# First conditioning round in two halves, the second among the first projections' products; later conditioning from the ninth load on

## The chip, the cores and the metric

One core of a Trainium2 chip runs the whole program. The metric is the time of one execution on the device in microseconds (us); lower is better. TensorE does matrix products, VectorE and ScalarE do element-wise work, GpSimd does a little, and SyncE issues nearly all transfers. Products are accumulated in PSUM, eight banks of 128 x 512 floats.

## The reference

A decoder trunk of two residual layers over 256 tokens of 1024 channels, in float32. Each layer computes a conditioning vector of 6 x 1024 values from c, `ada = silu(c) @ ada_w[l] + ada_b[l]`, split into shift, scale and gate for the token mixer and for the channel mixer, and then:

```
h = rmsnorm(x, norm_mix_g[l]) * (1 + sc1) + sh1
x = x + g1 * token_mixer(h, ...)
h = rmsnorm(x, norm_ffn_g[l]) * (1 + sc2) + sh2
x = x + g2 * (swiglu(h) if l is even else moe_swiglu(h))
```

The token mixer multiplies h by one wide matrix w_in (nine projections side by side, the first 512 columns being the queries hq of a gated linear recurrence and the next 512 its forget gates hf). It runs the recurrence and a differential softmax attention on the results, projects each of them, weighs them with sigmoid gates and applies w_out. The channel mixer is a dense SwiGLU in layer 0 and a choice of 2 out of 8 experts in layer 1.

## The kernel before

Activations lie transposed: a tile holds 128 channels by 256 tokens, and eight such channel blocks (k = 0 to 7) make the 1024 channels. To keep float32 accuracy at the faster fp32r rate, each operand is split into a high part (ScalarE copy, `wh`, `hh`) and a low part (VectorE difference, `wl`, `hl`), and three products are formed for each pair (`three`, L157). The helper `split` (L146, L148) does that for the weights, 1024 columns at a time. `load` (L120 and L123) fetches 1 MB of weights into one of six `raw` buffers, over SyncE's queue.

Conditioning (`ada_steps`) is done in rounds of 2048 columns, three for each layer. Round (0, 0) gives shift and scale of layer 0's token mixer. A round reads eight blocks of 1 MB, block k holding the rows p * 8 + k of the weights. A block is either multiplied on TensorE with silu(c) as the stationary operand ("t" in the table `ADA`) or accumulated on VectorE ("v", L219 and L221). The last block is followed by a copy of the result row, transposes and the addition of the bias, which turn it into columns. Round (0, 0) is all on TensorE, and its 512 result columns lie in two banks of 256 so that the first half can be finished a little earlier than the second. Even so all eight blocks must have arrived before either half is complete.

While round (0, 0) goes on, x is loaded between the first blocks, transposed (L370, L371), squared and summed (L261, L263, L271), and scaled by the inverse norm (L389). When the round is done, `norm_T` forms high and low parts of h (L299 to L301), and the mixer starts. Its steps come in the order of the string `ORDER`: first "r", the queries' projection, then "f", the forget gates' (both by `proj_T`: two loads each of 8 x 128 x 256 weights, all eight channel blocks accumulated for a group of 128 columns before the next group), then "s", the recurrence's scores (L530 to L565), "i", "q", "k", "g", "v" (projections by `proj_N`, two loads each), the attention "a" and "b", the recurrence's output "o", and four gates "0" to "3". The two branch projections and w_out follow.

The later conditioning rounds are cut into steps, the `fillers`. After each load of the mixer, `fill` may take one of them: the table `DELAYS` says after how many loads the first is taken, `RATES` every how many loads one is taken after that. Layer 0's mixer has 26 such loads, and 17 fillers: the attention's lambdas, and the rounds (0, 1) and (0, 2) of eight steps each. With a delay of 2 they fall on loads 2 to 18. The gate of round (0, 1) and the scale of round (0, 2) are needed when the outputs of w_out are evacuated. The first round does not count its blocks as such loads.

The program is not run in the order in which it is written. A scheduler with a model of the times orders the instructions of each engine, and the order on each queue is then fixed. `issue_after` ties a transfer to come no earlier than a given load in that order; `first_load` lists the mixer's loads from the first on.

Of the kernel before, what the change touches and what calls it, by code (L numbers as in the profile page):

```python
# [8 lines left out]
F32 = mybir.dt.float32  # L9
# [8 lines left out]
P = 128  # L18
D = 1024
# [24 lines left out]
DELAYS = (2, 8, 4, 0)  # L44
# [4 lines left out]
def hybrid_trunk(ctx: ExitStack, tc: tile.TileContext, x, c, ada_w, ada_b, norm_mix_g, norm_ffn_g, w_in, lb_logits,  # L49
# [43 lines left out]
    def ms():  # L93
        return msp.tile([P, 512], F32, tag="ms", name=nm("ms"))
# [97 lines left out]
    def ada_steps(l, r):  # L192
# [5 lines left out]
        halves = 2 if (l, r) == (0, 0) else 1  # L198
# [85 lines left out]
    def norm_T(rb, gain, sc, sh, xr=None):  # L284
# [4 lines left out]
        for part in ((0, 1), (2, 3)) if xr else ((0, 1, 2, 3),):  # L289
            js = slice(part[0], part[-1] + 1)  # L290
            gv, scv, av = (q.rearrange("p (h i) -> p h i", i=4)[:, :, js] for q in (gm, sc, gain))
            v_.scalar_tensor_tensor(gv, scv, 1.0, av, op0=ALU.add, op1=ALU.mult)
            for k in [4 * h + i for h in range(2) for i in part]:
                h, i = k // 4, k % 4
                hi, lo = hs[h], ls[h]
                val = small([P, S], "val", pool=prep)
                if xr:
                    x_ = xr[h][:, i, :]
                    s_.activation(hi[:, i, :], x_, AF.Identity, bias=sh[:, k:k + 1], scale=gm[:, k:k + 1])  # L299
                    v_.tensor_scalar(val, x_, gm[:, k:k + 1], sh[:, k:k + 1], op0=ALU.mult, op1=ALU.add)  # L300
                    v_.tensor_tensor(lo[:, i, :], val, hi[:, i, :].bitcast(F32), op=ALU.subtract)  # L301
                    continue
                v_.scalar_tensor_tensor(val, xT[h][:, i, :], gm[:, k:k + 1], rb[:, :S], op0=ALU.mult, op1=ALU.mult)
                s_.activation(hi[:, i, :], val, AF.Identity, bias=sh[:, k:k + 1])
                v_.scalar_tensor_tensor(lo[:, i, :], val, sh[:, k:k + 1], hi[:, i, :].bitcast(F32),
                                        op0=ALU.add, op1=ALU.subtract)
        return hs, ls
# [54 lines left out]

    ada = {}
    steps, ada[0, 0] = ada_steps(0, 0)

    def turn_x(t):
        for j in range(2):
            ps = ms()
            for k in range(4):
                t_.transpose(ps[:, k * P:(k + 1) * P], x_in[t][:, (j * 4 + k) * P:(j * 4 + k + 1) * P], ident)  # L370
            v_.tensor_copy(xT[j][:, :, t * P:(t + 1) * P], ps.rearrange("p (k t) -> p k t", k=4))  # L371

    pcol = const.tile([P, R_ALL], F32, name="pcol")
    for n, f in enumerate(steps):
        f()
        if n < NT:
            nc.sync.dma_start(x_in[n], x[0, n * P:(n + 1) * P, :])
            if n:
                nc.sync.dma_start(brows, ada_b.rearrange("l (k p) -> (l k) p", p=P))
        elif n < 2 * NT:  # L380
            turn_x(n - NT)
        elif n == 2 * NT:
            acc = []
            for k in range(KD):
                add_square(acc, k)
            rb = norm_rows(acc)
            xr = [w4("xr").rearrange("p (k t) -> p k t", k=4) for _ in range(2)]
            for k in range(KD):
                v_.tensor_tensor(xr[k // 4][:, k % 4, :], xT[k // 4][:, k % 4, :], rb[:, :S], op=ALU.mult)  # L389
        elif n == 2 * NT + 1:  # L390
            pps = ms()
            t_.transpose(pps[:, :R_QN], rows, ident[:R_QN, :R_QN])
            t_.transpose(pps[:, P:P + 96], brows, ident[:96, :96])
            v_.tensor_copy(pcol[:, :R_QN], pps[:, :R_QN])
            v_.tensor_copy(bcol, pps[:, P:P + 96])
# [54 lines left out]
    def mixer(l, norm, early, rb):  # L450
# [15 lines left out]

        def forget():

            def ev_f(g, ps):
                z, b = scaled(ps)  # L470
                s_.activation(f[:, g, :], z, AF.Sigmoid, bias=b)
                if z is not ps:
                    b = small([P, 1], "zn")
                    v_.tensor_scalar(b, ps[:, S:S + 1], -1.0, None, op0=ALU.mult)
                s_.activation(kq[:, g, :], z, AF.Sigmoid, bias=b, scale=-1.0)
                if l > 0:
                    v_.tensor_scalar(f[:, g, :], f[:, g, :], lbp[:, 0, g:g + 1], lbp[:, 1, g:g + 1], op0=ALU.mult, op1=ALU.add)
                    v_.tensor_scalar(kq[:, g, :], kq[:, g, :], lbp[:, 0, g:g + 1], None, op0=ALU.mult)
            proj_T(W, C_HF, *parts(True), KD, ev_f, 512)
# [8 lines left out]
        def reader():  # L488
            def ev_q(g, ps):
                z, b = scaled(ps)  # L490
                s_.activation(q[:, g, :], z, AF.Identity, bias=b)
            proj_T(W, C_HQ, *parts(True), KD, ev_q, 512,
                   None if l else (0, 1, 4, 5, 2, 3, 6, 7))
# [816 lines left out]
```

## Time and profile before

| | us |
|---|---|
| median of 3 runs | 1531.02 (1530.73 to 1533.77) |
| the profiled execution | 1531.64 |
| its span, first to last instruction | 1528.1 |
| TensorE busy | 1478.0 (97%) |
| VectorE busy | 625.4 (41%) |
| ScalarE busy | 374.2 (24%) |

The 3.5 us between the profiled execution's time and its span lie outside the recorded instructions. Busy time of TensorE counts overlapping, pipelined matmuls; where it is full, the distance between the starts of two matmuls tells its pace. An fp32 matmul is recorded as two, so the 32 matmuls that one pass over the blocks of half a conditioning round needs appear as 64. "Idle before" in brackets is the time that an engine stood still ahead of a row, and behind the arrow is what ended it. Slices in the first 40 us contain the whole of the stretch that the change edits.

### The profile page before, as it was taken

How to read it: one execution, taken by the hardware profiler on the slowest of the kernel's cores; microseconds unless marked ns; L12 is line 12 of the kernel's file. 1: busy time of each engine (PE TensorE's matmuls, PEld its weight loads, DVE VectorE, ACT ScalarE, POOL GpSimd, SP SyncE). 2: the span in 40 equal slices, each digit the busy share in tenths (PEclk: the TensorE clock that was granted, in tenths of full speed). 3: DMA queues.
4: the chain of work that ended last, by engine and by line, in shares of the span. 5: the costliest groups of instructions: out<-in, count | busy, mean ns of one | idle time of the engine just before them, and what ended most of it. 6: DMA issues, size and time to landing. Idle time of an engine off the chain costs nothing. (4 is left out here: it accounts for less than half of the span.)

```text
span 1528.1 us, 29828 instructions
## 1 busy us (share of the span) xinstructions
PE 1478.0 (97%) x12747; PEld 903.9 (59%) x12747; DVE 625.4 (41%) x1028; ACT 374.2 (24%) x618; POOL 36.1 (2%) x34
## 2 busy tenths in 40 slices
PE   5999999999999999999997999999999999999997
PEld 3988999999998899863342423433433434334332
DVE  4898777877688787630112111111021020110111
ACT  3535556544455455310000000000000000000000
POOL 1020100000000110000000000000000000000000
PEclk7999999999999999999998999999999999999999
DMA  9988545678796656869998999999999999999996
GB/s 355 368 302 282 188 140 165 221 241 303 267 333 227 198 186 200 315 244 366 379 363 337 411 417 412 413 415 414 415 414 412 411 418 409 410 415 409 410 413 262
DMA packets 184480, 506.63 MB, mean 332 GB/s; under 512 B 10872, under 2 KB 79108, under 8 KB 167700
## 3 DMA queue, kind: packets, MB, share of 16 engines
q1 hardware_dynamic: 184020, 504.55, 86.5%
q8 instruction: 102, 1.67, 0.4%
q14 instruction: 38, 0.31, 0.1%
q0 software_dynamic: 320, 0.09, 0.0%
HBM read 503.56 MB, written 1.05 MB: 330 GB/s over the span
## 5 line engine op out<-in xcount | busy, mean ns | idle before, releaser
L1064 PE MATMUL mm<-raw,X 128*32 128x512 f32 (+1 forms) x3888 | 440.0, 541 | 6.8 <-PEq L1165 6.4
L1064 PEld LDWEIGHTS mm<-raw,X 128*32 128x32 f32 x3888 | 134.0, 110 | 230.7 <-issue 190.1
L148 DVE TENSOR_TENSOR wl<-raw,wh 128x1024 fp32r<-128x1024 f32 (+1 forms) x188 | 227.1, 1212 | 73.1 <-ACT wh L146 70.8
L146 ACT ACTIVATE wh<-raw 128x1024 fp32r<-128x1024 f32 (+1 forms) x188 | 196.6, 1048 | 174.9 <-PE mm L157 131.6
L1104 PE MATMUL pd<-raw,u 128*32 128x512 f32 x1664 | 214.6, 594 | 2.1 <-DMA raw<-in_moe_w_dram 2.1
L1072 DVE TENSOR_TENSOR sa<-sa,mm 128x512 f32<-128x512 f32 (+1 forms) x32 | 19.9, 621 | 446.9 <-PE mm L1064 397.5
L157 PE MATMUL mm<-hh,wh 128*128 128x256 f32 x576 | 163.9, 285 | 3.3 <-ACT wh L146 3.1
L157 PE MATMUL mm<-hl,wh 128*128 128x256 f32 x576 | 164.5, 286 | 0.0
L157 PE MATMUL mm<-hh,wl 128*128 128x256 f32 x576 | 164.2, 285 | 0.1
L1069 PE MATMUL at<-raw,X 128*32 128x512 f32 (+1 forms) x968 | 161.6, 540 | 0.0
L1071 ACT ACTIVATE sa<-mm 128x512 f32<-128x512 f32 (+1 forms) x32 | 17.4, 544 | 493.8 <-PE mm L1064 476.4
L1104 PEld LDWEIGHTS pd<-raw,u 128*32 128x32 f32 x1664 | 57.3, 110 | 114.3 <-issue 103.6
L157 PEld LDWEIGHTS mm<-hh,wh 128*128 128x128 f32 x576 | 109.7, 190 | 5.6 <-ACT wh L146 3.4
L157 PEld LDWEIGHTS mm<-hl,wh 128*128 128x128 f32 x576 | 109.2, 190 | 0.7 <-issue 0.7
L157 PEld LDWEIGHTS mm<-hh,wl 128*128 128x128 f32 x576 | 109.0, 189 | 0.4 <-DVE wl L148 0.4
L1110 PE MATMUL pd<-raw,u 128*32 128x512 f32 x408 | 84.9, 592 | 0.0
L1069 PEld LDWEIGHTS at<-raw,X 128*32 128x32 f32 x968 | 44.0, 110 | 61.7 <-issue 56.9
L221 DVE SCALAR_TENSOR_TENSOR raw<-raw,cs,raw 128x2048 f32<-128x2048 f32 x32 | 75.1, 2348 | 10.7 <-DMA raw<-in_ada_w_dram 10.7
L1088 ACT ACTIVATE u<-ms 128x512 f32<-128x512 f32 (+1 forms) x32 | 17.4, 544 | 229.7 <-PE ms L1086 229.7
L157 PE MATMUL mm<-wh,hh 128*128 128x512 f32 x160 | 64.6, 404 | 0.0
L157 PE MATMUL mm<-wl,hh 128*128 128x512 f32 x160 | 64.0, 400 | 0.0
L157 PE MATMUL mm<-wh,hl 128*128 128x512 f32 x160 | 63.2, 395 | 0.0
(294 smaller groups left out, 1977.2 us busy)
## 6 DMA issues: line engine op xcount, KB each, us to landing
raw<-in_moe_w_dram SPq DMA_DIRECT2D x240, 1024.0 KB, 14.8
raw<-in_moe_w_dram SPq DMA_DIRECT2D x152, 512.0 KB, 11.4
raw<-in_ada_w_dram SPq DMA_DIRECT2D x47, 1024.0 KB, 5.2
raw<-in_w_in_dram SPq DMA_DIRECT2D x44, 1024.0 KB, 7.5
raw<-in_ffn_w_dram SPq DMA_DIRECT2D x30, 1024.0 KB, 5.3
xT<-in_moe_w_dram SPq DMA_DIRECT2D x40, 512.0 KB, 15.9
raw<-in_w_out_dram SPq DMA_DIRECT2D x8, 1024.0 KB, 5.4
raw<-in_w_branch_a_dram SPq DMA_DIRECT2D x4, 1024.0 KB, 5.1
```

The source lines that it names most:

```text
L146: s_.activation(wh[:, c], r[:, c], AF.Copy)
L148: v_.tensor_tensor(wl[:, c], r[:, c], wh[:, c].bitcast(F32), op=ALU.subtract)
L157: t_.matmul(ps, lhsT=lhs, rhs=rhs, start=first and i == 0, stop=last and i == 2)
L221: v_.scalar_tensor_tensor(got["acc"], raw, cs[:, k:k + 1], got["acc"], op0=ALU.mult, op1=ALU.add)
L1064: t_.matmul(ups[m][q:q + 32, :n], lhsT=xp[:, k, 32 * s:32 * s + 32], rhs=rhs[m][h], start=k == 0, stop=k == KD - 1)
L1069: t_.matmul(ups[2][q:q + 32, :n], lhsT=xp[:, k, 64:96], rhs=rhs[m][h], start=k == 0, stop=k == KD - 1)
L1071: s_.activation(sa[:, :n], ups[0][:, :n], AF.Silu)
L1072: v_.tensor_tensor(sa[:, :n], sa[:, :n], ups[1][:, :n], op=ALU.mult)
L1088: (v_.tensor_copy(dst, ps) if i_ else s_.activation(dst, ps, AF.Copy))
L1104: t_.matmul(dns[0][q:q + 32, :], lhsT=us[0][:, k, 64 * h + 32 * s:64 * h + 32 * s + 32], rhs=rhs[h][c], start=first and h == 0, stop=last ...
L1110: t_.matmul(dns[1][q:q + 32, :], lhsT=us[1][:, k, 32 * h:32 * h + 32], rhs=rhs[h][c], start=first, stop=last)
```

## The change

Round (0, 0) is no longer made by `ada_steps`. A generator `first_round(half)` makes one half of it: 512 channels of shift and the same 512 of scale, in four steps of two blocks of 512 KB (rows of 2 KB). It multiplies them on TensorE, turns the result into columns, forms the gain and also h's high and low parts for those four channel blocks. The first half is run ahead of the mixer. x is loaded first, before any conditioning weights. Its norm is now taken from the untransposed x (squares summed along the channels by ScalarE), x is scaled there (`xn`), and both x and the scaled x are transposed.

The second half is run inside the mixer's first step. Queries and forget gates of layer 0 are projected together: eight column groups lie in four PSUM banks, and the loop goes over the channel blocks, two for each load of 128 x 2 x 1024 weights. After given groups of blocks 1, 2 and 3 a step of the second half follows; blocks 4 to 7 use its result. The step "f" keeps only its constant loads for layer 0.

`DELAYS` for layer 0's mixer goes from 2 to 9, so that the 17 fillers fall on loads 9 to 25. Three small constants of the expert layer are held behind the ninth of the mixer's loads.

```diff
-DELAYS = (2, 8, 4, 0)
+DELAYS = (9, 8, 4, 0)
...
-    ada = {}
-    steps, ada[0, 0] = ada_steps(0, 0)
...
+    def first_round(half):
+
+        acc = adp.tile([P, 512], F32, tag="ada", name=nm("ada"))
+        src = ada_w[0].rearrange("(p k) (a h f) -> p k a h f", k=KD, h=2, f=512)
+        for i in range(4):
+            raw = rawp.tile([P, 2048], F32, tag="raw", name=nm("raw"))
+            for k in range(2):
+                nc.sync.dma_start(raw[:, k * 1024:(k + 1) * 1024].rearrange("p (a f) -> p a f", a=2), src[:, 2 * i + k, 0:2, half, :])
+            for k in range(2):
+                for q in range(4):
+                    t_.matmul(acc[32 * q:32 * q + 32, :256], lhsT=csr[:, 2 * i + k, :], rhs=raw[:, k * 1024 + q * 256:k * 1024 + (q + 1) * 256],
+                              start=i == 0 and k == 0, stop=i == 3 and k == 1)
+            yield
+        row, ps = small([P, 512], "row", pool=keep, bufs=1), ms()
+        v_.tensor_copy(row[:, :256], acc[:, :256])
...
+        v_.scalar_tensor_tensor(gm00[:, ks], col[:, 8 + 4 * half:12 + 4 * half], 1.0, pcol[:, R_MIX + 4 * half:R_MIX + 4 * half + 4], op0=ALU.add, op1=ALU.mult)
+        for i in range(4):
+            k = 4 * half + i
+            hi, lo, x_, val = first_hs[half][:, i, :], first_ls[half][:, i, :], xr[half][:, i, :], small([P, S], "val", pool=prep)
+            s_.activation(hi, x_, AF.Identity, bias=col[:, k:k + 1], scale=gm00[:, k:k + 1])
+            v_.tensor_scalar(val, x_, gm00[:, k:k + 1], col[:, k:k + 1], op0=ALU.mult, op1=ALU.add)
+            v_.tensor_tensor(lo, val, hi.bitcast(F32), op=ALU.subtract)
...
+    for t in range(NT):
+        nc.sync.dma_start(x_in[t], x[0, t * P:(t + 1) * P, :])
...
+    for t in range(NT):
+        s_.activation(xn[t], x_in[t], AF.Square, accum_out=x_sq[:, t:t + 1])
+    rstd(x_r, x_sq, D, NT)
...
+    steps = first_round(0)
...
         def reader():
...
+            xh, xl = parts()
+            banks = [mm() for _ in range(3)] + [at()]
+            ps = [bank[:, i * S:(i + 1) * S] for bank in banks for i in range(2)]
+            for k in range(KD):
+                if k == 0:
+                    steps = first_round(1)
+                if k % 2 == 0:
+                    raw = load(cols_src(W, k, C_HQ, 2, 1024), k=2)
+                    fill()
+                wh, wl = split(raw[:, k % 2 * 1024:(k % 2 + 1) * 1024])
+                for g in (4, 5, 0, 1, 6, 7, 2, 3):
+
+                    three(ps[g], xh[k // 4][:, k % 4, :], xl[k // 4][:, k % 4, :], wh[:, g * P:(g + 1) * P], wl[:, g * P:(g + 1) * P],
+                          k == 0 and g % 2 == 0, k == KD - 1 and g % 2 == 1, True)
+                    if (k, g) in ((1, 3), (2, 1), (2, 3), (3, 1)):
+                        next(steps)
+                        if k == 3:
+                            for _ in steps:
+                                pass
+                    if k == KD - 1 and g % 2:
+                        for g_ in (g - 1, g):
+                            (ev_q if g < 4 else ev_f)(g_ % 4, ps[g_])
...
     def late_constants():
-        nc.sync.dma_start(upper, k_upper)
-        nc.sync.dma_start(iota, k_iota)
-        nc.sync.dma_start(router, moe_router[0].rearrange("(k p) e -> p k e", p=P))
+        with tc.issue_after(first_load[8]):
+            nc.sync.dma_start(upper, k_upper)
+            nc.sync.dma_start(iota, k_iota)
+            nc.sync.dma_start(router, moe_router[0].rearrange("(k p) e -> p k e", p=P))
```

## Rows read from the trace of the kernel before

**Rows 1.** The page's 40 slices of 38 us: TensorE busy, and its clock.

```profile
PE   5999999999999999999997999999999999999997
PEclk7999999999999999999998999999999999999999
```

**Rows 2.** Stages: busy us and instructions per engine, PEclk, DMA share, GB/s.

```profile
0.00:35.00 35.00, 19.72 (x163) 9.62 (x163) 13.96 (x50) 9.12 (x18) 6.20 (x15) 0.82 0.98 352
35.00:61.00 26.00, 25.20 (x191) 24.41 (x192) 21.80 (x25) 16.96 (x26) 0.00 (x0) 0.91 1.04 394
61.00:165.00 104.00, 104.00 (x639) 87.18 (x638) 88.55 (x110) 46.27 (x73) 9.77 (x4) 1.00 0.82 289
165.00:230.00 65.00, 63.10 (x524) 61.13 (x522) 50.73 (x91) 34.19 (x67) 5.77 (x4) 1.00 0.47 153
620.00:1528.00 908.00, 876.24 (x8198) 348.28 (x8197) 140.99 (x300) 66.26 (x118) 0.69 (x1) 0.98 0.97 389
```

**Rows 3.** Waits of the first 36 us: total us, times, longest.

```profile
PE ada L227 <- DMA raw<-in_ada_w_dram: 12.4, 7, 6.4
```

**Rows 4.** Transfers of 0 to 62 us in 40 slices of 1.55 us.

```profile
GB/s 0 98 375 377 427 420 382 424 428 418 423 418 423 332 317 381 360 351 349 349 347 348 348 373 429 404 348 367 410 392 371 423 399 400 391 425 394 395 408 425
```

**Rows 5.** Timeline 6 to 36 us: start, us, engine, line, op.

```profile
6.40 1.08 PE L227 MATMUL ada<-raw,csr 128*32 128x256 f32 x8 [6.40 <-DMA raw<-in_ada_w_dram]
...
14.36 0.64 PE L227 MATMUL ada<-raw,csr 128*32 128x256 f32 x8 [0.91 <-DMA raw<-in_ada_w_dram]
...
14.82 0.61 PE L227 MATMUL at<-raw,csr 128*32 128x256 f32 x8
...
19.35 1.08 PE L227 MATMUL ada<-raw,csr 128*32 128x256 f32 x8 [0.45 <-DMA raw<-in_ada_w_dram]
...
29.84 1.08 PE L227 MATMUL at<-raw,csr 128*32 128x256 f32 x8 [0.23 <-DMA raw<-in_ada_w_dram]
...
31.98 2.08 ACT L299 ACTIVATE hh<-xr,col,gm 128x256 fp32r<-128x256 f32 x4 [5.90 <-DVE gm L292]
...
33.96 1.99 ACT L146 ACTIVATE wh<-raw 128x1024 fp32r<-128x1024 f32 x2
...
35.05 0.58 PE L157 MATMUL mm<-hh,wh 128*128 128x256 f32 x1 [2.69 <-ACT wh L146]
```

**Rows 6.** Timeline of SyncE's queue: an issue among the conditioning blocks.

```profile
7.98 0.33 SPq L1182 DMA_DIRECT2D upper<-in_k_upper_dram  x1
```

**Rows 7.** Timeline of TensorE, 37 to 62 us: the first projections' products.

```profile
37.49 0.41 PE L157 MATMUL mm<-hh,wl 128*128 128x256 f32 x1
37.71 0.41 PE L157 MATMUL mm<-hl,wh 128*128 128x256 f32 x1
...
39.81 0.28 PE L157 MATMUL mm<-hh,wh 128*128 128x256 f32 x1
39.93 0.29 PE L157 MATMUL mm<-hh,wl 128*128 128x256 f32 x1
...
58.17 0.39 PE L157 MATMUL mm<-hh,wh 128*128 128x256 f32 x1 [0.28 <-ACT kq L475]
...
61.12 1.05 PE L542 MATMUL ms<-q,kq 128*128 128x128 f32 x8
```

**Rows 8.** Timeline of ScalarE, 57 to 59 us: evacuations of the forget gates.

```profile
58.00 0.39 ACT L471 ACTIVATE f<-mm 128x256 f32<-128x256 f32 x1
58.26 0.41 ACT L475 ACTIVATE kq<-mm 128x256 f32<-128x256 f32 x1
```

**Rows 9.** Timelines: a conditioning accumulation on VectorE; TensorE at the attention's end.

```profile
49.05 2.35 DVE L221 SCALAR_TENSOR_TENSOR raw<-raw,cs,raw 128x2048 f32<-128x2048 f32 x1
...
206.75 0.87 PE L433 MATMUL at<-ident,od 128*128 128x128 f32 x6 [1.45 <-DVE od L640]
```

**Rows 10.** Windows of 10 us, columns as in rows 2: the clock.

```profile
20.00:30.00 10.00, 6.89 (x64) 2.93 (x58) 4.21 (x18) 0.21 (x1) 0.00 (x0) 0.67 1.07 350
30.00:40.00 10.00, 6.84 (x32) 4.68 (x29) 8.88 (x28) 7.83 (x12) 0.00 (x0) 0.52 1.08 372
```

More of the change, by code (lines that the diff above doesn't have):

```diff
@@ L282, in norm_rows, with norm_T @@
         return rb
-    def norm_T(rb, gain, sc, sh, xr=None):
+    def norm_T(rb, gain, sc, sh):
         gm = small([P, KD], "gm", pool=keep)
         hs, ls = ([w4(n, F32R, "h").rearrange("p (k t) -> p k t", k=4) for _ in range(2)] for n in ("hh", "hl"))
[L289 to L306, printed above, removed]
+        v_.scalar_tensor_tensor(gm, sc, 1.0, gain, op0=ALU.add, op1=ALU.mult)
+        for k in range(KD):
+            h, i = k // 4, k % 4
+            hi, lo = hs[h], ls[h]
+            val = small([P, S], "val", pool=prep)
+            v_.scalar_tensor_tensor(val, xT[h][:, i, :], gm[:, k:k + 1], rb[:, :S], op0=ALU.mult, op1=ALU.mult)
+            s_.activation(hi[:, i, :], val, AF.Identity, bias=sh[:, k:k + 1])
+            v_.scalar_tensor_tensor(lo[:, i, :], val, sh[:, k:k + 1], hi[:, i, :].bitcast(F32),
+                                    op0=ALU.add, op1=ALU.subtract)
         return hs, ls
@@ L360, in residual_T @@
         return acc, evac
-    ada = {}
-    steps, ada[0, 0] = ada_steps(0, 0)
-    def turn_x(t):
-        for j in range(2):
[L368 to L395, printed above, removed]
@@ new lines, in hybrid_trunk @@
+    ada = {(0, 0): {"done": True, "tile": const.tile([P, 4, 4], F32, name="col00")}}
+    ada[0, 0]["col"] = ada[0, 0]["tile"].rearrange("p q j -> p (q j)")
+    pcol = const.tile([P, R_ALL], F32, name="pcol")
+    first_hs, first_ls = ([w4(n, F32R, "h").rearrange("p (k t) -> p k t", k=4) for _ in range(2)] for n in ("hh", "hl"))
+    gm00 = small([P, KD], "gm", pool=keep)
+    xr = [w4("xr").rearrange("p (k t) -> p k t", k=4) for _ in range(2)]
+    def first_round(half):
[12 more added lines that the diff above has]
+        v_.tensor_copy(row[:, :256], acc[:, :256])
+        for j in range(2):
+            t_.transpose(ps[:, j * P:(j + 1) * P], row[:, j * P:(j + 1) * P], ident)
+        dst, bias = (q.rearrange("p (a h) (c j) -> p h a c j", h=2, j=2)[:, half]
+                     for q in (ada[0, 0]["tile"], bcol[:, :16].rearrange("p (q j) -> p q j", j=4)))
+        for c in range(2):
+            v_.tensor_tensor(dst[:, :, c], ps[:, :2 * P].rearrange("p (j a c r) -> p c a j r", j=2, a=2, c=2)[:, c, :, :, 0], bias[:, :, c], op=ALU.add)
+        col, ks = ada[0, 0]["col"], slice(4 * half, 4 * half + 4)
+        v_.scalar_tensor_tensor(gm00[:, ks], col[:, 8 + 4 * half:12 + 4 * half], 1.0, pcol[:, R_MIX + 4 * half:R_MIX + 4 * half + 4], op0=ALU.add, op1=ALU.mult)
[5 more added lines that the diff above has]
+            v_.tensor_tensor(lo, val, hi.bitcast(F32), op=ALU.subtract)
@@ new lines, in turned_x @@
+    def turned_x(src, dst, t, j, copy):
+        ps = ms()
+        for k in range(4):
+            t_.transpose(ps[:, k * P:(k + 1) * P], src[:, (j * 4 + k) * P:(j * 4 + k + 1) * P], ident)
+        copy(dst[j][:, :, t * P:(t + 1) * P], ps.rearrange("p (k t) -> p k t", k=4))
+    for t in range(NT):
+        nc.sync.dma_start(x_in[t], x[0, t * P:(t + 1) * P, :])
+    nc.sync.dma_start(brows, ada_b.rearrange("l (k p) -> (l k) p", p=P))
+    x_sq, x_r = small([P, NT], "x_sq", pool=keep, bufs=1), small([P, NT], "x_r", pool=keep, bufs=1)
@@ new lines, in hybrid_trunk @@
+    xn = [w4("xn", tag="g") for _ in range(NT)]
+    for t in range(NT):
+        s_.activation(xn[t], x_in[t], AF.Square, accum_out=x_sq[:, t:t + 1])
+    rstd(x_r, x_sq, D, NT)
+    for t in range(NT):
+        if t:
+            s_.activation(xn[t], x_in[t], AF.Copy, scale=x_r[:, t:t + 1])
+        else:
+            v_.tensor_scalar(xn[t], x_in[t], x_r[:, t:t + 1], None, op0=ALU.mult)
+    for j in range(2):
+        for t in range(NT):
+            turned_x(x_in[t], xT, t, j, v_.tensor_copy)
@@ L397, in hybrid_trunk @@
+    steps = first_round(0)
+    next(steps)
+    for j in range(2):
+        for t in range(NT):
+            turned_x(xn[t], xr, t, j, (lambda o, i: s_.activation(o, i, AF.Copy)) if t else v_.tensor_copy)
+    pps = ms()
+    t_.transpose(pps[:, :R_QN], rows, ident[:R_QN, :R_QN])
+    t_.transpose(pps[:, P:P + 96], brows, ident[:96, :96])
+    v_.tensor_copy(pcol[:, :R_QN], pps[:, :R_QN])
+    v_.tensor_copy(bcol, pps[:, P:P + 96])
+    for _ in steps:
+        pass
     pps = ms()
@@ L1220, in hybrid_trunk @@
                 rb = in_sbuf(norm_rows(acc))
-            y = mixer(l, lambda: norm_T(rb, pcol[:, R_MIX + 8 * l:R_MIX + 8 * l + 8], col[:, 8:16], col[:, 0:8], None if l else xr),
-                      early if l else None, rb)
+            y = mixer(l, lambda: norm_T(rb, pcol[:, R_MIX + 8 * l:R_MIX + 8 * l + 8], col[:, 8:16], col[:, 0:8]) if l else (first_hs, first_ls),
+                      early if l else None, rb if l else None)
         while fillers:
```

40 lines of the change are left out of this document (23 added, 17 removed).

## The prediction

> **What bounds the kernel now.** I read the page's slices first, because the edit touches only the start of a long program, and one has to know whether time saved there lasts to the end. TensorE is busy in nine tenths or more of nearly every slice after the first, in which it is busy for half and its clock is at seven tenths [rows 1]. The table by stage says the same in figures: in the first 35 us TensorE works 19.7 us while the DMA share is 0.98; from 61 to 165 us it is busy without a gap at full clock; to 230 us it lacks 1.9 us of 65; in the expert stage, from 620 us on, DMA share is 0.97 at 389 GB/s [rows 2]. So there are three regimes: a start bound by transfers, a middle bound by TensorE, an end bound by the experts' weights. The transfers of the end are issued as buffers come free, in the order of the program, and nothing in them is tied to an absolute time. Whatever the first projections gain or lose is therefore passed on to the end in full, unless the middle opens a gap.
>
> Next the waits of the start: TensorE waited 12.4 us for the conditioning weights, seven times [rows 3]. The DMA slices confirm that this is bandwidth and not latency: from 6 us on nearly every slice moves 317 to 428 GB/s, about 425 where 8 KB rows of conditioning weights stream alone, about 348 where 1 KB rows of w_in do [rows 4]. The timeline then gives the path: conditioning block 0 is used at 6.40 us, block 2 at 14.36, block 4 at 19.35, the last half of block 7 at 29.84; the first normalised channels start at 31.98, the first weight split at 33.96, the first projection product at 35.05 [rows 5]. The last of the 192 products of queries and forget gates is done when the scores begin, at 61.12 [rows 7]. These two times, 35.05 and 61.12, are what the edit can move.
>
> **The change part by part.** The sum is made against the profiled execution: span 1528.1, time 1531.64 us, 0.6 us above the median shown.
>
> *Half the weights ahead of the first product.* Shift and scale of the first 512 channels need 4 MB instead of 8. x (1 MB) now goes first and takes the place that block 0 had: there by about 6.4 us. Then four loads of 1 MB. Two blocks took 4.99 us from 14.36 to 19.35, 2.5 us each [rows 5]. The new loads have 2 KB rows, which no row shows; between the 425 GB/s of 8 KB rows and the 348 of 1 KB rows [rows 4] a load takes 2.5 to 3.0 us, and I take 2.75: the fourth lands at 17.4 (16.4 to 18.4). The small constants that were issued at 7.98 [rows 6], amid the conditioning blocks, are now held behind the ninth weight load, which helps to keep to that.
>
> From the last conditioning load to the first product the chain before took 35.05 - 29.84 = 5.2 us (products, row copy, transposes, bias, gain, four ACT normalisations, one split) [rows 5]. The new one has the same steps, with 16 conditioning matmul records instead of 8 behind the last load: 0.4 us more. So the first product is at 23.0 (21.0 if the split goes ahead of three of the four normalisations, 24.4 with slow rows). Gain at this point: 35.05 - 23.0 = 12.0 us. The new work on x (two squares and scalings, eight more transposes, four more copies) lies between 7 and 15 us, when VectorE and ScalarE have time: they were busy 14.0 and 9.1 of the first 35 us [rows 2]. If that cover failed, each microsecond beyond 17.4 would be paid.
>
> *The other half among the products.* Its 64 matmul records now stand in TensorE's queue between projection products, where there was waiting before. Sixteen of them took 14.36 to 15.43, 1.07 us at full clock, and some 2 us at the lower level (1.08 for eight) [rows 5]: four groups cost 4.3 us, at most 8. Are the weights there in time? The second half's last load is the eleventh MB: 6.4 + 10 x 2.75 = 33.9 (31.4 to 36.4). TensorE gets to it after 84 of the 192 products. Before, the first product came at 35.05, products then followed each other at 0.21 us, and from 39.81 at 0.12, the full clock, after some 16 of them [rows 7]. With the same 4.8 us of slow start the sum is 23.0 + 4.8 + 68 x 0.12 + 3 x 1.07 = 39.2. So the transfers are ahead by about 3 us, and TensorE bounds this stretch. Behind it come row copy, transposes, bias, gain and one normalisation, some 2 us, of which the 12 products left in block 3 cover 1.4: a gap of about 0.5 us.
>
> *Merged projections.* The same 192 products, now channel block by channel block into four PSUM banks, with the evacuations at the end. Twelve ACT evacuations start 0.26 us apart [rows 8], 3.1 us, of which the last block's 24 products (2.9 us) hide most; the value projection behind them needs the first bank first. I take 0, the bounds are -0.4 (the stall at 58.17 [rows 7] goes) and +2. I take the -0.3 of that stall as gained.
>
> Sum at the end of the projections: -12.0 + 4.3 + 0.5 - 0.3 = -7.5 us.
>
> *Later conditioning.* Seven loads' worth of VectorE accumulations, 2.35 us each [rows 9], leave loads 3 to 9 and follow load 18, in the last gates and the branch products. VectorE was idle for 14.3 us of 165 to 230 us [rows 2], and 16.5 us arrive. But in 61 to 165 us it had 15.5 us idle and loses several of these accumulations, so the recurrence's levels, which precede the attention in its queue, move forward and vacate room. TensorE did not wait in that earlier stretch, so nothing is gained there. I take 0 for both; the bounds are -1.9, all of TensorE's wait in that stretch, around the attention's last transposes at 206.75 [rows 9], and +4.8 (rival B). Of the w_out evacuations, which need these results, none comes before load 25's own work by less than a block of products.
>
> So the profile would be 1524.1, and the median 1531.0 - 7.5 = 1523.5 us; the likeliest case's own range is 1520 to 1527.
>
> The Trainium skill, "DMA: Bandwidth & Descriptors", section "Where 436 GB/s comes from", says that about 358 GB/s on the HBM side binds such loads. By it a load takes 2.9 us and the first product comes 0.7 us later, -6.8 in the sum. The trace shows slices up to 428 GB/s, so I keep to the trace.
>
> **The rivals.**
>
> *A. Transfers and order do better.* The split goes ahead of the normalisations, loads keep 2.5 us, and TensorE is soon at full clock: first product at 21.0, four groups at 4.3, no gap, and the half-clock stretch (16 products at 0.09 extra) gone: -14.0 + 4.3 - 0.3 - 1.4 = -11.4: 1519.6. For it: the clock was at 1.0 in part of the start. Against it: it was 0.67 and 0.52 between 20 and 40 us [rows 10], where TensorE worked piecemeal.
>
> *B. VectorE becomes the bound at the mixer's end.* If nothing moves forward, 16.5 us of accumulations meet 14.3 us of idle time, and the part of it before 170 us, some 2.6 us, is out of reach: 4.8 us over, and the splits behind them hold up TensorE. -7.5 + 4.8 = -2.7: 1528.3. For it: TensorE's longest wait of that stretch is there already. Against it: the accumulations can slip into w_out's four loads.
>
> *C. The clock stays at its lower level (slower).* TensorE starts its products while the weights still arrive. If it waits for them again and again, its clock stays at 1.2 GHz, as it was granted between 20 and 40 us, when the engine alternated between work and waits for DMA [rows 10]. Blocks 0 to 3 then cost 80 x 0.09 = 7.2 us more and the conditioning groups 3.7 more; if blocks 4 to 7 stay low too, another 8.6. Together 19.5 - 7.5 = +12.0: 1543. The first two alone give +3.4: 1534.4. It decides from about 83 products at the lower level. Against it: by the sum above TensorE, not the transfers, is late, and dense products brought the clock up within 5 us before. The Trainium skill, "TensorE: Matmul & The Clock Gate", section "HAM oscillation — how this bites in real kernels", speaks for it: bursts of matmuls between DMA waits fall back to half rate at each wait. The drop between 20 and 40 us agrees with it.
>
> *D. The change does not do what it says.* The order on the queues is not the program's: constants of a much later stage were issued at 7.98 us [rows 6]. If the second half's matmuls or loads are put ahead of the first products, the first product waits for 33.9 + 5.2 = 39.1, and with 192 x 0.12 + 3 behind it the end is at 65: +4. With only part of it put ahead, nothing changes: 1531.
>
> **How the numbers follow.** Forecast 0.56; A 0.16; B 0.14; C 0.07; D 0.07, half of it slower and half without effect. A measurement of this kernel tells a change from none at about 0.2%, 3.1 us: faster means under 1528.0. B lies on that line and I split it: faster 0.56 + 0.16 + 0.07 = 0.79; same 0.07 + 0.04 = 0.11; slower 0.07 + 0.03 = 0.10. The range goes from A with TensorE's 1.9 us of waits in the tail gone and the projections' stalls better by another 1, 1516.5, to past B, 1530: it leaves out C and most of D.
>
> **What would show it.** The first projection product at 21 to 24.4 us; sixteen-record groups of conditioning between products, waiting for no DMA; a gap of under 1 us ahead of channel block 4; clock at 1.0 by about 30 us; the first score product at 53 to 55; after 61 us as few TensorE gaps as before. I am wrong if the first product is later than 27 us, if TensorE waits for conditioning weights among the products, if the clock there stays near 0.5, or if gaps of more than 2 us in all appear around the branch products.

## The result: slower, and the profile after

The changed kernel takes 1542.84 us (median of 6 runs, 1540.86 to 1545.45) against 1533.4 us for the kernel before (6 runs, 1530.73 to 1534.01): ratio 1.006, 95% interval 1.0046 to 1.0075. It is 9.4 us slower; 1523.5 had been forecast, and the range ended at 1530. The profiled execution took 1543.61 us with a span of 1541.8.

The page's first slice is now busier and at a higher clock, as forecast. The second, the sixth and the last are a tenth less busy than before, and the rest looks as before but for a tenth of the clock [rows 1].

```profile
PE   7899989999999999999997999999999999999996
PEclk9999999999999999999997999999999999999998
```

The table by stage, columns as in [rows 2], tells where in time that is.

```profile
0.00:35.00 35.00, 24.82 (x195) 16.35 (x196) 15.51 (x41) 13.61 (x19) 6.30 (x15) 0.90 0.97 356
35.00:61.00 26.00, 21.64 (x169) 19.46 (x169) 11.59 (x19) 12.55 (x20) 0.00 (x0) 0.87 1.02 369
61.00:165.00 104.00, 103.34 (x649) 89.65 (x650) 85.91 (x110) 47.90 (x80) 9.43 (x4) 1.00 0.70 246
165.00:230.00 65.00, 60.14 (x468) 55.46 (x465) 53.38 (x86) 29.91 (x58) 5.94 (x4) 0.95 0.62 217
```

TensorE works 5.1 us more in the first 35 us, then gives 3.6 us back up to 61 us, and from 165 to 230 us it lacks 4.9 us instead of 1.9, at a lower clock. Four marks, read off both timelines, place the loss: the first projection product moved from 35.05 to 23.46 us, the first scores only from 61.12 to 60.60, the channel mixer's first activation from 260.5 to 265.7, and the first of the last four accumulations of the experts' output from 1521.3 to 1535.1. So the start's gain was gone by 61 us, 5.7 us were lost in the mixer, and 8.6 us behind it. These are single profiled executions, whose spans lie 13.7 us apart where the medians lie 9.4 apart: the places are sure, the sizes are taken from the experiments.

**Up to the scores.** TensorE's wait for conditioning weights in the first 36 us fell from 12.4 us [rows 3] to 3.7. Of the 12.4, 6.4 were the wait for the very first block, in whose place TensorE now waits 5.6 us for `ident` and x; the fall that counts is from 6.0 to 3.7:

```profile
PE ada L370 <- DMA raw<-in_ada_w_dram: 3.7, 3, 2.3
```

TensorE's timeline (start, us, engine, line, operation, in brackets the idle time before it and what ended it) shows the first product, the last of the groups of the second half at 39.01 (the two before it are at 33.76 and 36.38), the transposes of its result, and then what was not forecast: one wait ahead of channel block 4 and one inside it, and products 0.21 us apart, the half clock, until 51.57.

```profile
23.46 0.79 PE L157 MATMUL mm<-hh,wh 128*128 128x256 f32 x2 [0.23 <-ACT wh L146]
...
39.01 1.07 PE L370 MATMUL ada<-raw,csr 128*32 128x256 f32 x16
...
41.55 0.38 PE L376 MATMUL ms<-ident,row 128*128 128x128 f32 x2
43.86 0.39 PE L157 MATMUL mm<-hh,wh 128*128 128x256 f32 x1 [1.93 <-ACT hh L386]
...
46.49 0.58 PE L157 MATMUL mm<-hl,wh 128*128 128x256 f32 x1 [1.32 <-DVE hl L388]
46.87 0.41 PE L157 MATMUL mm<-hh,wh 128*128 128x256 f32 x1
47.09 0.41 PE L157 MATMUL mm<-hh,wl 128*128 128x256 f32 x1
...
51.57 0.34 PE L157 MATMUL mm<-hh,wl 128*128 128x256 f32 x1
51.74 0.28 PE L157 MATMUL mm<-hl,wh 128*128 128x256 f32 x1
...
60.60 1.16 PE L598 MATMUL ms<-q,kq 128*128 128x128 f32 x8 [1.10 <-ACT q L509]
```

A good part of the cause stands in VectorE's timeline. It did nothing for 9.72 us, and then had two weight splits, 2.35 us, between the copy of the result row and the columns, and two more between the gain and the low parts `hl`.

```profile
40.15 0.42 DVE L374 COPY row<-ada 128x256 f32<-128x256 f32 x1 [9.72 <-PE ada L370]
40.49 2.35 DVE L148 TENSOR_TENSOR wl<-raw,wh 128x1024 fp32r<-128x1024 f32 x2
42.76 0.22 DVE L380 TENSOR_TENSOR col<-ms,bcol 128x4 f32<-128x4 f32 x2
43.01 0.16 DVE L382 SCALAR_TENSOR_TENSOR gm<-col,pcol 128x4 f32<-128x4 f32 x1
43.09 1.23 DVE L148 TENSOR_TENSOR wl<-raw,wh 128x1024 fp32r<-128x1024 f32 x1
44.23 0.73 DVE L387 TENSOR_SCALAR val<-xr,gm,col 128x256 f32<-128x256 f32 x2
44.88 1.22 DVE L148 TENSOR_TENSOR wl<-raw,wh 128x1024 fp32r<-128x1024 f32 x1
46.02 0.75 DVE L388 TENSOR_TENSOR hl<-val,hh 128x256 fp32r<-128x256 f32 x2
```

The first two could not come earlier: their weights, channel blocks 4 and 5, are behind the second half on the queue, as the wait of ScalarE, which makes the high parts, shows.

```profile
38.16 2.00 ACT L146 ACTIVATE wh<-raw 128x1024 fp32r<-128x1024 f32 x2 [10.19 <-DMA raw<-in_w_in_dram]
```

The rest of the cause is in TensorE's own queue: the row copy starts at 40.15 and takes 0.42 us, but the transposes stand behind the last 12 products of block 3 and start at 41.55.

**The mixer's end.** The waits of TensorE from 165 to 230 us (total, times, longest) come to 4.6 us. The first is the wait of [rows 9], which was 1.45 us in the kernel before, where TensorE waited 2.0 us in all in this stretch:

```profile
PE at L462 <- DVE od L696: 3.4, 1, 3.4
PE at L689 <- DVE pr L686: 0.8, 1, 0.8
PE ms L693 <- DVE ol L466: 0.4, 1, 0.4
```

VectorE's timeline shows late accumulations of 2.35 us among the attention's work; the last block's maximum comes at 197.00 us, where it came at 190.68 before. First the lines of after, then that of before:

```profile
182.54 2.35 DVE L221 SCALAR_TENSOR_TENSOR raw<-raw,cs,raw 128x2048 f32<-128x2048 f32 x1 [0.50 <-DMA raw<-in_ada_w_dram]
...
188.68 2.35 DVE L221 SCALAR_TENSOR_TENSOR raw<-raw,cs,raw 128x2048 f32<-128x2048 f32 x1
...
197.00 1.21 DVE L673 TENSOR_REDUCE mx<-pr 128x4 f32<-128x1024 f32 x1
```

```profile
190.68 1.22 DVE L617 TENSOR_REDUCE mx<-pr 128x4 f32<-128x1024 f32 x1
```

After the wait of 3.4 us the clock is at 0.72 of full in the window from 210 to 220 us:

```profile
210.00:220.00 10.00, 9.77 (x62) 9.37 (x63) 4.41 (x10) 3.77 (x6) 0.00 (x0) 0.72 0.09 30
```

**The experts.** From 850 to 1500 us the transfers (last column, GB/s) run at 413 before and 408 after. First the row of before, then that of after:

```profile
850.00:1500.00 650.00, 645.23 (x6164) 238.22 (x6160) 86.87 (x162) 39.39 (x71) 0.00 (x0) 1.00 1.02 413
```

```profile
850.00:1500.00 650.00, 642.18 (x6084) 237.54 (x6076) 87.09 (x163) 39.41 (x71) 0.00 (x0) 1.00 1.02 408
```

TensorE is busy nearly throughout in both; the lower rate uses up the lead of the transfers, and is paid late, nearly all of it as waits for weights from 1440 us on. Before:

```profile
PE pd L1104 <- DMA raw<-in_moe_w_dram: 2.1, 2, 1.2
PE mm L1064 <- DMA raw<-in_moe_w_dram: 0.5, 1, 0.5
```

After:

```profile
PE pd L1160 <- DMA raw<-in_moe_w_dram: 5.0, 4, 1.4
PE mm L1120 <- DMA raw<-in_moe_w_dram: 2.4, 4, 0.8
```

The same bytes are moved by the same instructions. What differs is where they go: the two new small tiles `x_sq` and `x_r` push everything allocated behind them by 64 bytes, and the compiled program places the weight buffers `raw` 96 bytes past a multiple of 512 in each partition, where it was 32. By its addresses this holds for 196 of the experts' 336 MB, which go to the `raw` and the split buffers; 120 MB go to a second group of buffers that lies 224 bytes further past such a multiple in every kernel here (256 before, 320 after), and 20 MB to two tiles that do not move.

### The profile page after: what moved, and what is told of

The parts are those of the page before. It is cut to its first block, busy times and chain, and to the rows that moved or that the text cites. A ratio compares the mean times of both kernels' runs of the same rounds, so it can differ in the third digit from the quotient of the medians.

```text
span 1541.8 us, 29829 instructions
## 1 busy us (share of the span) xinstructions
PE 1483.3 (96%) x12751; PEld 906.8 (59%) x12751; DVE 620.3 (40%) x1019; ACT 373.7 (24%) x615; POOL 36.0 (2%) x34
## 5 line engine op out<-in xcount | busy, mean ns | idle before, releaser
L1120 PE MATMUL mm<-raw,X 128*32 128x512 f32 (+1 forms) x3888 | 447.4, 542 | 9.0 <-PEq L1221 6.6
L1160 PE MATMUL pd<-raw,u 128*32 128x512 f32 x1664 | 219.6, 597 | 6.6 <-DMA raw<-in_moe_w_dram 6.6
L1125 PE MATMUL at<-raw,X 128*32 128x512 f32 (+1 forms) x968 | 166.6, 540 | 0.0
L157 PE MATMUL mm<-hh,wh 128*128 128x256 f32 x560 | 160.2, 286 | 2.2 <-ACT hh L386 1.9
L157 PE MATMUL mm<-hl,wh 128*128 128x256 f32 x560 | 160.2, 286 | 1.3 <-DVE hl L388 1.3
L157 PE MATMUL mm<-hh,wl 128*128 128x256 f32 x560 | 160.0, 286 | 0.0
L1127 ACT ACTIVATE sa<-mm 128x512 f32<-128x512 f32 (+1 forms) x32 | 17.4, 544 | 491.7 <-PE mm L1120 465.4
L1166 PE MATMUL pd<-raw,u 128*32 128x512 f32 x408 | 85.5, 592 | 0.0
L1144 ACT ACTIVATE u<-ms 128x512 f32<-128x512 f32 (+1 forms) x32 | 17.4, 544 | 240.2 <-PE ms L1142 240.2
```

Of the source, the lines that this page charges most:

```text
L157: t_.matmul(ps, lhsT=lhs, rhs=rhs, start=first and i == 0, stop=last and i == 2)
L1120: t_.matmul(ups[m][q:q + 32, :n], lhsT=xp[:, k, 32 * s:32 * s + 32], rhs=rhs[m][h], start=k == 0, stop=k == KD - 1)
L1125: t_.matmul(ups[2][q:q + 32, :n], lhsT=xp[:, k, 64:96], rhs=rhs[m][h], start=k == 0, stop=k == KD - 1)
L1127: s_.activation(sa[:, :n], ups[0][:, :n], AF.Silu)
L1144: (v_.tensor_copy(dst, ps) if i_ else s_.activation(dst, ps, AF.Copy))
L1160: t_.matmul(dns[0][q:q + 32, :], lhsT=us[0][:, k, 64 * h + 32 * s:64 * h + 32 * s + 32], rhs=rhs[h][c], start=first and h == 0, stop=last ...
```

## The experiments

The theories, as they were put down ahead of the first four runs: **T**, the delay of 9 loads costs 3 to 5 us at the mixer's end; **P**, the place of the weight buffers costs the experts 8 to 11 us; and the halving itself gains. The rival to both is that the halving loses by itself. All ratios are to the kernel before, with their 95% intervals. It was measured anew beside each set of runs, at 1533.4 us beside the changed kernel and at 1532.5 to 1532.8 beside the others, so a difference to the changed kernel carries up to 0.9 us. "Place" is the distance of the `raw` buffers from a multiple of 512 bytes, the rate is that of 850 to 1500 us.

| run | reader | delay | place | GB/s | us | ratio |
|---|---|---|---|---|---|---|
| kernel before | before | 2 | 32 | 413 | 1532.5 to 1533.4 | |
| changed kernel | halves | 9 | 96 | 408 | 1542.84 | 1.006 (1.0046 to 1.0075) |
| e1 | before | 2 | 96 | 408 | 1538.86 | 1.0051 (1.0029 to 1.0073) |
| e2 | halves | 9 | 32 | 413 | 1537.19 | 1.0035 (1.0018 to 1.0053) |
| e3 | before | 9 | 32 | 413 | 1538.72 | 1.0034 (1.0021 to 1.0047) |
| e4 | halves | 2 | 96 | 408 | 1532.42 | 0.9997 (0.9985 to 1.001) |
| e5 | halves | 2 | 32 | 413 | 1525.45 | 0.9946 (0.9928 to 0.9963) |
| e6 | halves | 2 | 0 | 415 | 1519.83 | 0.9917 (0.9893 to 0.9941) |
| e7 | halves, load moved | 2 | 32 | 413 | 1526.48 | 0.9963 (0.9947 to 0.9979) |
| e9 | before | 2 | 96 | 408 | 1539.1 | 1.0035 (1.0021 to 1.0048) |
| e10 | before | 2 | 0 | 415 | 1528.42 | 0.997 (0.9956 to 0.9985) |
| e11 | halves | 2 | 128 | 408 | 1533.57 | 1.0005 (0.999 to 1.002) |
| e12 | halves | 2 | 64 | 408 | 1534.08 | 1.0014 (1.0 to 1.0028) |

**e1, the kernel before with 64 bytes of padding.**

```diff
     v_.memset(mhalf, -0.5)
+    pad = small([P, 16], "pad", pool=keep, bufs=1)
+    g_.memset(pad, 0.0)
```

> The kernel before with one unused tile of 64 bytes per partition in the pool of long-lived small tiles, which moves every later tile, the weight buffers among them, 64 bytes up: to where the changed kernel has them (96 past a multiple of 512 instead of 32). Its instructions are otherwise the same. Theory P (the experts' weights arrive more slowly into buffers at the moved addresses): the expert stage moves 1 to 1.5% fewer GB/s, and the time is 8 to 11 us over the kernel before. Rival Q (the expert stage's rate differs for another reason: the execution, the order of loads): within 2 us of the kernel before, some 413 GB/s between 900 and 1500 us as there.

Sixteen unused floats cost 6.3 us. The rate falls as P expected; the time grows by less than its 8 to 11 us. Its waits for weights from 1440 us on:

```profile
PE pd L1106 <- DMA raw<-in_moe_w_dram: 6.5, 4, 2.7
PE mm L1066 <- DMA raw<-in_moe_w_dram: 1.1, 2, 0.8
```

**e2, the changed kernel with 448 bytes of padding** (`[P, 112]` in the same place): back to 32.

> The changed kernel with an unused tile of 448 bytes, which puts the weight buffers 32 bytes past a multiple of 512 again, as in the kernel before. Theory P: about 10 us faster than the changed kernel, 1531 to 1535, GB/s in the expert stage back by 1 to 1.5%. Rival Q: 1541 to 1545 as the changed kernel.

The rate is back at 413 and 5.7 us of the loss are gone, where 10 had been expected. P holds in both directions, in a smaller size than expected.

**e3, the kernel before with delay 9.**

```diff
-DELAYS = (2, 8, 4, 0)
+DELAYS = (9, 8, 4, 0)
```

> The kernel before with the later conditioning moved to loads 9 to 25 alone; buffers at the old addresses. Theory T (late accumulations on VectorE hold up the last attention block, and TensorE waits and restarts at half clock around 206 us): 3 to 5 us over the kernel before, with a TensorE wait of over 3 us ahead of the attention's last transposes. Rival U (the tail's loss comes from the new start, not from the delay): within 1.5 us of the kernel before. By P the expert stage keeps its old GB/s.

With the delay alone it takes 6.1 us more than the kernel before, where T expected 3 to 5. The scores come at 61.20, as before, the channel mixer begins at 266.5 us, 6.0 late, and TensorE's waits of 165 to 230 us stand where those of the changed kernel do:

```profile
PE at L433 <- DVE od L640: 3.4, 1, 3.4
PE ms L637 <- DVE ol L437: 1.8, 1, 1.8
PE at L633 <- DVE pr L630: 0.8, 1, 0.8
```

**e4, the changed kernel with delay 2** (the same line, the other way).

> The changed kernel with the later conditioning back at loads 2 to 18; buffers as in the changed kernel. Theory T: the wait at 206 us shrinks to that of the kernel before, 3 to 5 us gained at the end of the mixer; but accumulation blocks now stand among the first projections' loads, which may cost up to 3 us there: 1538 to 1543. Rival U: no gain at the end of the mixer. By P the expert stage keeps the lower GB/s of the changed kernel.

10.4 us faster than the changed kernel, and faster than the 1538 to 1543 that were expected. The waits of 165 to 230 us are nearly those of before:

```profile
PE at L462 <- DVE od L696: 1.4, 1, 1.4
PE mm L157 <- ACT oh L465: 0.5, 1, 0.5
```

The scores also come 3.2 us sooner, at 57.39. With delay 2 the filler's first load goes ahead of channel blocks 6 and 7, so their splits don't stand ahead of the low parts; the wait for `hl` is 0.24 us instead of 1.32, and the half clock ends at 48.3:

```profile
44.04 0.39 PE L157 MATMUL mm<-hh,wh 128*128 128x256 f32 x1 [2.16 <-ACT hh L386]
...
45.58 0.58 PE L157 MATMUL mm<-hl,wh 128*128 128x256 f32 x1 [0.24 <-DVE hl L388]
...
48.31 0.35 PE L157 MATMUL mm<-hl,wh 128*128 128x256 f32 x1
48.49 0.28 PE L157 MATMUL mm<-hh,wh 128*128 128x256 f32 x1
```

The cost of up to 3 us that was expected of accumulations among the first loads did not appear; the scores came earlier. So in the changed kernel the delay cost twice, in the mixer's end and ahead of the scores. Against e1, at the same place, the halves are worth 1538.86 - 1532.42 = 6.4 us.

**e5, halves, delay 2, 448 bytes of padding.**

> The changed kernel with layer 0's delay back at 2 and 448 bytes of padding, so that the weight buffers begin 32 bytes past a multiple of 512 again, as before the change. If the two losses found (the late accumulations and the buffers' place) are all that speaks against the halves, their gains add: first 620 us as in e4 (scores at 57.4, first expert product at 664.4), experts at 412 to 414 GB/s, time 1532.4 - 6 = 1525 to 1527 us, ratio 0.995 to 0.997. Rival: the place of the buffers costs something only where the experts start late, and the two don't add: 1530 to 1533.

It beats the kernel before by 7.1 us (1532.52 in that comparison): the two losses do add. From the changed kernel to e5 it is 17.4 us, by way of e4 as 10.4 + 7.0, by way of e2 as 5.7 + 11.7; counted against the kernel before that was measured beside each, it is 16.5.

**e6, the same with 416 bytes** (`[P, 104]`): the `raw` and split buffers on a multiple of 512 (the second group 224 past one).

> As the run before, but with 416 bytes of padding: the weight buffers begin on a multiple of 512. If what matters is the distance from a multiple of 512, and small is good, the rate is 413 GB/s or more and the time 1523 to 1527. If 32 is a lucky place and others are like 96, the rate is 407 to 409 and the time 1531 to 1533.

The fastest of all, 12.7 us under the kernel before, and under the 1523 to 1527 that were expected for a small distance. From 1440 us on no wait for weights is left in TensorE's list. The rate:

```profile
850.00:1500.00 650.00, 644.62 (x6178) 239.36 (x6174) 87.37 (x163) 39.98 (x73) 0.00 (x0) 1.00 1.02 415
```

**e7, an earlier load**, on top of e5. It asks whether VectorE's pile-up at 40 us or the arrival of the weights sets the gap ahead of block 4.

```diff
-            with tc.issue_after(first_load[2]) if not l else nullcontext():
+            with tc.issue_after(first_load[3]) if not l else nullcontext():
...
-                    raw = load(cols_src(W, k, C_HQ, 2, 1024), k=2)
+                    raw = raws[k] if k in raws else load(cols_src(W, k, C_HQ, 2, 1024), k=2)
...
                     if (k, g) in ((1, 3), (2, 1), (2, 3), (3, 1)):
+                        if k == 3:
+                            raws[4] = load(cols_src(W, 4, C_HQ, 2, 1024), k=2)
                         next(steps)
```

> Delay 2 and 448 bytes of padding as above, and the load of w_in's channel blocks 4 and 5 issued ahead of the second half's last load (alibi one load later). Theory 1, the pile-up: VectorE stands idle from 31.7 to 40.1 us and then has the splits of blocks 4 and 5 ahead of the columns; with the splits done by 38 the columns follow the row at once, and the scores come 1 to 2.5 us earlier than the 57.4 of e4. Theory 2, the arrival: the transfers are full up to 40 us, the second half's last weights come 2.6 us later in exchange, its last group is at 41.5 and the first product of block 4 at 44.0 to 44.5 as before; scores within 0.7 us of 57.4.

The second theory, in the main: the scores come at 58.24 us, no earlier than in e4 (57.39) and e5 (57.92), though a little beyond the 0.7 us that it allowed. The splits now end at 39.7, and the columns follow the row with nothing between, but the last group comes at 40.93 and the first product of block 4 at 44.13:

```profile
37.36 2.36 DVE L148 TENSOR_TENSOR wl<-raw,wh 128x1024 fp32r<-128x1024 f32 x2 [4.91 <-ACT wh L146]
42.07 0.42 DVE L376 COPY row<-ada 128x256 f32<-128x256 f32 x1 [2.35 <-PE ada L372]
43.02 0.23 DVE L382 TENSOR_TENSOR col<-ms,bcol 128x4 f32<-128x4 f32 x2 [0.53 <-PE ms L378]
```

```profile
40.93 1.07 PE L372 MATMUL ada<-raw,csr 128*32 128x256 f32 x16
42.55 0.44 PE L378 MATMUL ms<-ident,row 128*128 128x128 f32 x2 [0.55 <-DVE row L376]
44.13 0.39 PE L157 MATMUL mm<-hh,wh 128*128 128x256 f32 x1 [1.15 <-ACT hh L388]
```

Both the second half and blocks 4 and 5 have to be in before block 4 can go, and the transfers are full until then (386 to 428 GB/s between 28 and 44 us in the two kernels). Between these two orders the gain of 1.7 us in the chain behind the last group is paid back by that group coming 1.9 us later. A third one, the loads as in the changed kernel with transposes and columns put ahead of the last products and the splits, was not tried; it might keep the 1.7 us.

**e8, short accumulations.**

```diff
-                    v_.scalar_tensor_tensor(got["acc"], raw, cs[:, k:k + 1], got["acc"], op0=ALU.mult, op1=ALU.add)
+                    n = 64 if l == 0 else 2048
+                    v_.scalar_tensor_tensor(got["acc"][:, :n], raw[:, :n], cs[:, k:k + 1], got["acc"][:, :n], op0=ALU.mult, op1=ALU.add)
```

> The changed kernel (delay 9), but layer 0's later conditioning rounds accumulate 64 of their 2048 columns on VectorE; the values of the rest are left wrong. All loads, their order and the buffers' count stay. If the loss at the mixer's end is the 2.35 us accumulations in VectorE's queue among the attention's work, the channel mixer's first activation moves from 265.7 to 255 to 259, at or near e4's 255.0, and TensorE is busy over 62.5 us of 165 to 230. If it is the loads that come late in the mixer (their place on SyncE's queue, the buffers they hold), it stays at 263 to 266.

This kernel leaves out 1984 of the 2048 columns of these accumulations, so that other tokens reach other experts later on; only its first 300 us are read. The channel mixer begins at 256.6 us instead of 265.7, and from 165 to 230 us TensorE has no gap at all:

```profile
165.00:230.00 65.00, 65.00 (x545) 62.08 (x544) 50.53 (x95) 33.62 (x64) 4.66 (x4) 1.00 0.72 243
```

The scores, at 60.8, are as late as in the changed kernel, so the 9.1 us lie behind them. The attention's last maximum comes at 180.69 us instead of 197.00. It is the accumulations, not the late loads, which it keeps. From the scores to the channel mixer it takes 195.7 us, less than the 199.4 of the kernel before, in which the accumulations have their full length too; so 9.1 is more than the mixer had lost.

**e9, only the weight buffers and what lies behind them (splits, the phases' own tiles) moved**: a pool of 64 bytes between the activations' pools and the weights'.

```diff
+    padp = ctx.enter_context(tc.tile_pool(name="padp", bufs=1))
     rawp = ctx.enter_context(tc.tile_pool(name="rawp", bufs=RAW_BUFS))
...
+    pad = padp.tile([P, 16], F32, name="pad")
+    g_.memset(pad, 0.0)
```

> The kernel before with 64 bytes between the activations' buffers and the weight buffers: the weight buffers and what lies behind them (splits, phases) move from 32 to 96 past a multiple of 512, the small tiles and the activations h, g and the experts' X stay. If it is the weight buffers' own place that sets the rate, as in e1: 407 to 409 GB/s from 850 to 1500 us, last expert segment 75 us, 1537 to 1540 us. Rival, the place of the activations that were moved with them in e1: 412 to 414 GB/s, 1530 to 1534 us.

As slow as e1, with h, g and the experts' X where they were, so the place of the activations is not the cause. The buffers that the experts' weights go to and the other tiles behind them are not told apart by it:

```profile
850.00:1500.00 650.00, 640.28 (x6060) 235.88 (x6052) 86.89 (x162) 39.41 (x71) 0.00 (x0) 1.00 1.02 408
```

**e10, the kernel before with 480 bytes** (`[P, 120]`): `raw` on a multiple of 512.

> The kernel before with 480 bytes of padding, the weight buffers on a multiple of 512 and nothing else changed. If place and halves are independent, the gain is e6's over e5: 5.6 us, 415 GB/s, 1526 to 1528 us, ratio 0.9955 to 0.998; the halves with delay 2 are then worth 6 to 8 us at this place too. If e6's gain came from an interplay with the halves, 1531 to 1534.

4.4 us faster than the kernel before without a change of its work, at the edge of what was expected. Against it the halves with delay 2 (e6) are worth 1528.42 - 1519.83 = 8.6 us.

**e11 and e12, halves with delay 2 at 128 and at 64** (`[P, 8]` and `[P, 120]`).

> The changed kernel with delay 2 and the weight buffers 128 bytes past a multiple of 512. If the period is 128 bytes or a divisor of it, it is like 0: 414 to 416 GB/s, 1518 to 1522 us. If it is 512 (the size of a part of a row), it is like 96 or worse: 405 to 409 GB/s, 1531 to 1534 us.

> The same with the weight buffers 64 bytes past a multiple of 512. If the period is 64 bytes, 32 and 96 would be alike, which e1 and e2 exclude, so it is not like 0 for that reason. If the rate falls steadily with the distance from a multiple of 128 or 512, it lies between 32 and 96: 410 to 412 GB/s, 1526 to 1531 us. If only 64-byte alignment and some further effect count, it is like 0: 415 GB/s, 1518 to 1522 us.

Both at 408 GB/s, both with the time of the kernel before. A multiple of 64 or of 128 is not enough, and the rate doesn't fall steadily with the distance: none of what was expected of e12 came true.

## Why the prediction was wrong

Three steps failed: the gap ahead of channel block 4 (0.5 us forecast, 5.4 measured), the later conditioning (0 forecast, 6.0 in e3), and the start's gain "passed on to the end in full", which left out that the moved buffers slow the experts down (no term, 5.7 to 6.3 in e2 and e1). Term by term:

- **First product, -12.0.** Right: 23.46 us for 23.0. The first half's last load was used at 18.14 us, a little later than the 17.4 forecast, and the chain behind it took 5.3 for 5.6.
- **Four groups of the second half, +4.3, and their weights in time.** Nearly right: the last three took 1.07 us each without a wait, the last one at 39.01 for 39.2. The first went in two parts of 1.08 us at the half clock, one of them at 22.15 us, ahead of the first product and behind a wait of 2.3 us for its weights, the other at 24.61.
- **A gap of 0.5 us ahead of block 4.** Wrong: 1.9, then 1.3, then some 24 products at the half clock, 24 x 0.09 = 2.2: 5.4 us. The chain after the last group was put at some 2 us, with 1.4 of them covered by block 3's last 12 products. It took 43.86 - 40.08 = 3.8 in the changed kernel and 44.13 - 42.00 = 2.1 in e7, where neither products nor splits stand in it. Of the 1.7 us between them, 0.9 are the transposes, which stand behind those 12 products in TensorE's queue (1.40 us after the start of the row copy, 0.48 in e7), so that the products cover little of the chain; and 0.7 are the splits of blocks 4 and 5, which stand between row and columns in VectorE's queue (columns 1.21 us after the transposes' start, 0.47 in e7). The prediction asked whether the second half's weights were in time, and did not ask it of w_in's next load, which stands behind them on the queue. The half clock is rival C's mechanism on a small scale: it followed one pair of waits, where rival C looked for it among blocks 0 to 3, which ran at full clock from 27.8 us. The Trainium skill, "TensorE: Matmul & The Clock Gate", section "HAM oscillation — how this bites in real kernels", says that bursts between waits fall back to half rate. The trace agrees at this place, with a delay: the eight products behind the wait of 1.9 us still ran at the full clock.
- **Evacuations, -0.3.** Wrong in sign, inside its bound of +2: TensorE waits 1.1 us ahead of the scores (60.60); in e4 it doesn't.
- **Later conditioning taken at 0.** The step that failed in the mixer. The place (rival B, "TensorE's longest wait of that stretch") was right, the size lay above rival B's bound of +4.8: in e3, where nothing else was changed, the channel mixer begins 6.0 us late, and TensorE's waits from 165 to 230 us grow from 2.0 to 6.0 (to 4.6 in the changed kernel); the half clock behind the longest adds to them. The reason for 0 was that accumulations "can slip" and leave room earlier. They can't: the order in VectorE's queue is fixed before it runs, and the accumulations of 2.35 us that stand ahead of the last attention block delay it, whatever idle time lies elsewhere. The sum of idle time was the wrong measure: in the changed kernel VectorE works only 2.7 us more in that stretch than before (53.4 for 50.7), not 16.5, and stands idle for 11.6 us of it, yet TensorE lacks 4.9. With the accumulations shortened (e8) it lacks nothing.
- **"Passed on to the end in full".** The step that failed for the rest. It is true of the order of the transfers, and not of their rate: by e1 and e2 the moved buffers cost 6.3 and 5.7 us, paid mostly in the last expert segment. Nothing in the profile of before could show that, but the new tiles were in the diff, and the prediction didn't ask what they push.
- **The sum.** The scores came at 60.60 us where the sum gives 61.12 - 7.5 = 53.6: 4.9 of these 7.0 us are the gap ahead of block 4 and its half clock, 1.4 the evacuations, 0.5 the first product. The halves alone were forecast at -7.5 and give -7.1 (e5), -6.4 (e4 against e1) and -8.6 (e6 against e10). That is partly by luck: the scores come at 57.4 to 57.9, where 53 to 55 was forecast, so some 3.5 us of it are gained up to there and the rest behind. From the scores to the channel mixer e4 takes 197.6 us and the kernel before 199.4; where these 1.8 us and those behind them come from was not tried.

## What to carry to other kernels

A change of several parts is timed part by part: here a gain of 7 us was hidden under a schedule constant that cost some 10 and a pair of tiny tiles that cost some 6. When work is put off into a later stretch, don't weigh it against the idle time there; look for the chain with a deadline that it will stand ahead of in its engine's queue. And where a stage lives on its transfers, compare the addresses of its buffers before and after, and run the old kernel with the new addresses.

## What the runs showed of the hardware

The rate of the experts' 1 MB and 512 KB loads depends on where in a partition they land: 415 GB/s with the `raw` buffers on a multiple of 512 bytes, 413 at 32 past it, and 408 at 64, 96 and 128 past it, in two kernels with the same transfers. Places 0, 32 and 96 were seen in both kernels, 64 and 128 in one. The tiles behind the buffers moved with them each time. The second group of buffers lies 224 bytes further, and with it the five places fit one rule: a buffer on a multiple of 256 is filled faster. At place 0 that is so for the 196 MB of `raw` and splits, at 32 for the 120 MB of the second group (at 256), at 64, 96 and 128 for neither. With 408 GB/s for the rest, both faster rates give an estimate of some 420 to 422 GB/s for the buffers on such a multiple (415 by 196 of 336 MB, 413 by 120). No run put all buffers on a multiple of 256, so the rule is a fit and not shown; the places above 128 stay open. Between 415 and 408 lie 1.7%, 11 us of 650; what of it arrives at the end depends on the lead that the transfers have: here 6 to 9 us between 413 and 408, and 4 to 6 between 415 and 413. The Trainium skill, "DMA: Bandwidth & Descriptors", section "Where 436 GB/s comes from", has some 358 GB/s on the HBM side as what binds; the measurement, 408 to 415 over 650 us, decides against it here.

A pause can be dearer than it looks: after 1.9 and 1.3 us of waiting, the next 24 or so products ran at the half clock and cost another 2.2 us; in e4, after 2.2 and 0.2 us, it was some 13 products. In both, the eight products between the two waits still ran at the full clock.
